# A convolution's last input load, issued later and with its last 16 partitions cut into short and long pieces

## Chip, cores and metric

The kernel runs on one core of one Trainium2 chip. The metric is device time in microseconds (us), median over executions; lower is better. A profiled span is about 1.7 us shorter than the same execution's time. A run is called slow, and left out of medians and ratios below, when it is over 1.5% above the fastest of its kernel.

## The reference

A 3x3 convolution, padding 1, 16 images of 64 channels and 64x64 pixels, 128 output channels, all float32; 9 of 10 weights are zero.

```python
x_pad = np.pad(x, ((0, 0), (0, 0), (pad, pad), (pad, pad)), mode='constant')
for b, co, ci, kh, kw in ...:            # five nested loops
    if weight[co, ci, kh, kw] != 0:
        output[b, co] += weight[co, ci, kh, kw] * x_pad[b, ci, kh:kh+h, kw:kw+w]
```

## The kernel before

Two images ("a pair") fill the 128 partitions: 64 channels each. GpSimd issues the loads of x, converted to bf16 on the way, all at the start; SyncE issues the stores. For each block of 16 image rows GpSimd (POOL in the profiles) makes a sum `s` (three buffers), PE, the matrix engine, multiplies, VectorE (DVE) adds and writes the output tile.

```python
nc.sync.dma_start(out=w_sb, in_=weight...)
nc.sync.dma_start(out=x_head[:, 0:HEAD, :], in_=pair(0)[:, 0:HEAD, :])
nc.gpsimd.dma_start(out=xs[0][:, HEAD:H, :], in_=pair(0)[:, HEAD:H, :])
...
for p in range(1, NP):                                   # NP = 8 pairs
    nc.gpsimd.dma_start(out=xs[p], in_=pair(p))
# ... weights, 27 idle matmuls, first conversions (cut)
for p in range(NP):
    o = [o_pool.tile([C_OUT, H, W], FP32, name="o") for _ in range(2)]
    last = p == NP - 1
    for blk in range(4):
        ...                                              # GpSimd, PE, ACT, VectorE
        if last and blk % 2 == 1:                        # last pair: stores by halves
            for n in range(2):
                rows = slice(r0 - 16, r0 + 16)
                nc.sync.dma_start(out=out[2 * p + n][:, rows, :], in_=o[n][:, rows, :])
    if not last:
        for n in range(2):
            nc.sync.dma_start(out=out[2 * p + n], in_=o[n])
```

## Time and profile before

| | before |
|---|---|
| time, median | 127.66 us (3 runs, 127.59 to 127.9) |
| profiled span | 125.4 us |
| PE's unbroken stretch | 7.12 to 109.21 us |
| last compute step ends | 111.76 us |
| last store lands | 124.20 us |

The row to read is the last one against the one above it: 12.4 us in which only DMA engines work. Two more lines of the page are needed later. The first counts packets of the DMA queues by size; those under 512 B are nearly all 4-byte completion increments. The second gives, for the seven whole loads of x, the size and the time from issue to landing:

```profile
DMA packets 4044, 42.93 MB, mean 342 GB/s; under 512 B 448, under 2 KB 448, under 8 KB 704
...
x<-in_x_dram POOLq DMA_DIRECT2D x7, 1024.0 KB, 29.3
```

### The profile page before, as it was taken

What the parts mean: (1) busy time and instruction counts of PE and PEld (TensorE: products, weight loads), DVE (VectorE), ACT (ScalarE), POOL (GpSimd) and SP (SyncE); (2) the same over time, 40 slices, a digit from 0 to 9 for tenths busy, and PEclk for the clock granted to TensorE, in tenths of its full rate; (3) what the DMA queues carried; (4) which work ended last, traced back from release to release, by engine and by line L of the source; (5) the groups of instructions that cost most, each with busy time, mean ns of one, the idle gap of its engine ahead of it and who ended that gap; (6) DMA issues with size and microseconds to landing.
All of it is one profiled execution on the core that took longest, in us unless ns stands there. A gap on an engine that the chain in (4) does not pass through costs nothing.

```text
span 125.4 us, 2486 instructions
## 1 busy us (share of the span) xinstructions
PE 107.5 (86%) x1002; PEld 58.8 (47%) x1002; DVE 82.4 (66%) x135; ACT 39.0 (31%) x71; POOL 40.7 (32%) x45
## 2 busy tenths in 40 slices
PE   6679999999999999999999999999999999920000
PEld 6435555555555555555555555555555555500000
DVE  0463877877787778777877787778777877760000
ACT  4555323333333333333333333333333333300000
POOL 6936533333333333333333333333333300000000
PEclk9999999999999999999999999999999999997555
DMA  5999999989999999999999999999999999999980
GB/s 146 338 222 220 212 214 220 191 259 350 324 311 337 308 293 319 342 316 308 426 429 423 408 429 434 450 416 434 418 418 429 429 444 423 434 397 423 423 369 10
DMA packets 4044, 42.93 MB, mean 342 GB/s; under 512 B 448, under 2 KB 448, under 8 KB 704
## 3 DMA queue, kind: packets, MB, share of 16 engines
q1 hardware_dynamic: 2880, 34.90, 66.2%
q0 software_dynamic: 1152, 7.86, 30.7%
q8 instruction: 8, 0.13, 0.4%
q14 instruction: 4, 0.03, 0.1%
HBM read 17.07 MB, written 33.55 MB: 404 GB/s over the span
## 4 chain that ended last, share of the span: by engine, by line
PE 81%; DMA 4%; DVE 1%; issue 1%; DVEq 0%; SPq 0%
PE ps L135 81%; DMA o<-in_x_dram 4%; DVE o L168 1%; DVEq L214 0%; DVE x L87 0%; SPq L60 0%; DVEq L168 0%
## 5 line engine op out<-in xcount | busy, mean ns | idle before, releaser
L168 DVE TENSOR_TENSOR o<-ps,pc 128x512 f32<-128x512 f32 x124 | 77.8, 686 | 22.1 <-PE ps L135 19.8
L135 PE MATMUL ps<-x,wT 64*128 64x504 bf16 (+3 forms) x780 | 88.8, 373 | 1.5 <-DVE x L87 1.5
L135 PEld LDWEIGHTS <-wT 64*128 64x128 bf16 x966 | 55.2, 94 | 49.4 <-issue 1.5
L154 POOL TENSOR_TENSOR s<-x 128x512 bf16<-128x512 bf16 x31 | 35.6, 1152 | 57.7 <-PE ps L135 41.5
L161 ACT COPY pc<-ps 128x512 f32<-128x512 f32 x62 | 33.3, 589 | 64.0 <-issue 61.8
L135 PE MATMUL ps<-s,wT 64*128 64x512 bf16 (+1 forms) x186 | 25.7, 377 | 0.0
L74 PE MATMUL ps<-idle_rhs 128*128 128x128 bf16 x27 | 3.1, 310 | 1.0 <-DVE idle_rhs L71 1.0
L67 POOL DMA_DIRECT2D x<-in_x_dram x7 | 3.7, 561 | 0.0
L74 PEld LDWEIGHTS <-idle_rhs 128*128 128x128 bf16 x27 | 2.8, 144 | 1.0 <-DVE idle_rhs L71 1.0
L91 DVE CAST w_bf<-w_sb 128x192 bf16<-128x192 f32 (+1 forms) x4 | 1.3, 382 | 3.0 <-DMA w_sb<-in_weight_dram 3.0
L149 DVE COPY o<-ps 128x512 f32<-128x512 f32 x2 | 1.4, 692 | 2.0 <-PE ps L135 2.0
L148 ACT COPY o<-ps 128x512 f32<-128x512 f32 x2 | 1.2, 586 | 2.4 <-PE ps L135 2.4
L87 ACT CAST x<-o 128x576 bf16<-128x576 f32 (+1 forms) x2 | 1.5, 802 | 0.5 <-DMA o<-in_x_dram 0.5
L91 ACT ACT_TABLE_LOAD x1 | 1.3, 1283 | 0.7 <-PEq L203 0.7
L97 PE MATMUL ps<-ident,w_bf 128*128 128x128 bf16 x9 | 1.1, 292 | 0.4 <-DVE w_bf L91 0.4
L87 DVE CAST x<-o 128x576 bf16<-128x576 f32 x1 | 0.5, 460 | 1.4 <-DMA o<-in_x_dram 1.4
L91 ACT CAST w_bf<-w_sb 128x64 bf16<-128x64 f32 (+1 forms) x2 | 0.7, 418 | 1.9 <-DMA w_sb<-in_weight_dram 1.9
L97 PEld LDWEIGHTS <-w_bf 128*128 128x128 bf16 x9 | 0.8, 128 | 0.8 <-DVE w_bf L91 0.8
L101 DVE TENSOR_TENSOR wT<-ps,wT 128x384 bf16<-128x384 f32 x2 | 1.0, 550 | 0.0
L63 POOL DMA_DIRECT2D x<-in_x_dram x1 | 0.7, 696 | 0.8 <-POOLq L203 0.8
L71 DVE MEMSET idle_rhs<- 128x64 uint32 x1 | 0.1, 112 | 0.8 <-PEq L203 0.8
L110 ACT CAST wT<-ps 128x384 bf16<-128x384 f32 x1 | 0.5, 481 | 0.4 <-PE ps L97 0.4
(8 smaller groups left out, 1.9 us busy)
## 6 DMA issues: line engine op xcount, KB each, us to landing
out_dram<-o SPq DMA_DIRECT2D x14, 2048.0 KB, 19.8
x<-in_x_dram POOLq DMA_DIRECT2D x7, 1024.0 KB, 29.3
out_dram<-o SPq DMA_DIRECT2D x4, 1024.0 KB, 12.3
o<-in_x_dram SPq DMA_DIRECT2D x1, 1024.0 KB, 5.4
x<-in_x_dram POOLq DMA_DIRECT2D x1, 512.0 KB, 7.5
w_sb<-in_weight_dram SPq DMA_DIRECT2D x1, 288.0 KB, 3.1
```

Of the source, the lines that this page charges most:

```text
L67: nc.gpsimd.dma_start(out=xs[p], in_=pair(p))
L74: nc.tensor.matmul(idle_ps, idle_rhs, idle_rhs, start=True, stop=True)
L87: copy(out=xs[0][:, a:b, :], in_=x_head[:, a:b, :])
L91: copy(out=w_bf4[:, g, a:b, :], in_=w_v[:, k : k + b - a, :])
L97: nc.tensor.matmul(wps[:, j, :], src, ident, start=True, stop=True)
L101: nc.vector.tensor_tensor(out=wT[:, g], in0=wps, in1=wT[:, G1], op=SUB)
L135: nc.tensor.matmul(ps[n][:, lo:hi, c_lo:c_hi], tap(g, kw, n), src[q, a:b:step, c_lo + kw - 1 : c_hi + kw - 1], start=(i == 0), stop=(i == ...
L148: nc.scalar.copy(out=o[0][:, r0 : r0 + rows, :], in_=ps[0])
L149: nc.vector.tensor_copy(out=o[1][:, r0 : r0 + rows, :], in_=ps[1])
L154: nc.gpsimd.tensor_tensor(out=s, in0=xs[p][:, r0 : r0 + 16 : 2, :], in1=xs[p][:, r0 + 1 : r0 + 16 : 2, :], op=ADD)
L161: nc.scalar.copy(out=c, in_=shared[n])
L168: nc.vector.tensor_tensor(out=o[n][:, first : r0 + 16 : 2, :], in0=ps[n], in1=pc[n], op=ADD)
```

## The change

The 16 DMA engines do not end together. As I read it, the change means to give engines 0 to 7 a little less of the last load and engines 8 to 15 a little more; it also issues this load later.

```diff
-    for p in range(1, NP):
+    for p in range(1, NP - 1):
         nc.gpsimd.dma_start(out=xs[p], in_=pair(p))
...
     for p in range(NP):
         o = [...]
+        if p == 2:
+            for c0, c1, a, b in (
+                (0, 112, 0, H),
+                (112, 120, 0, 8),
+                (112, 120, 8, H),
+                (120, 128, 0, 8),
+                (120, 128, 8, H),
+            ):
+                nc.gpsimd.dma_start(
+                    out=xs[NP - 1][c0:c1, a:b, :], in_=pair(NP - 1)[c0:c1, a:b, :]
+                )
```

## The prediction

> **What bounds the kernel now.** I read the page's slices first, then the chain that ended last, then stretches by stage, then the data queues at the end. The slices show two things busy from start to finish: the PE and the transfers. Only one of them reaches the end.
>
> ```profile
> span 125.4 us, 2486 instructions
> ...
> PE   6679999999999999999999999999999999920000
> ...
> DMA  5999999989999999999999999999999999999980
> ...
> q1 hardware_dynamic: 2880, 34.90, 66.2%
> q0 software_dynamic: 1152, 7.86, 30.7%
> ```
>
> PE falls idle in slice 36 of 40 (about 110 us); the 16 DMA engines stay at nine tenths or more two to three slices longer. The two queues, q1 (stores, and the first two loads) and q0 (the other loads of x, converted to bf16 on the way), take 66.2% + 30.7% = 96.9% of all 16 engines' time over the whole span. The chain of waits agrees: its last compute step is a VectorE add that ends at 111.16 + 0.60 = 111.76 us, though the span is 125.4; what follows is only the landing of stores.
>
> ```profile
> 7.12 102.09 PE ps L135 x954
> ...
> 111.16 0.60 DVE o L168
> ```
>
> By stage (columns: stretch, its length, busy time of each engine, granted clock, DMA share, GB/s):
>
> ```profile
> 25.00:53.00 28.00, 28.00 (x264) 14.98 (x262) 21.72 (x36) 9.30 (x18) 10.10 (x9) 1.00 1.01 317
> 63.00:109.00 46.00, 46.00 (x432) 24.58 (x430) 35.81 (x58) 16.10 (x30) 13.84 (x12) 1.00 1.01 429
> 112.00:122.00 10.00, 0.00 (x0) 0.00 (x0) 0.00 (x0) 0.00 (x0) 0.00 (x0) 0.63 0.97 409
> 122.00:125.40 3.40, 0.00 (x0) 0.00 (x0) 0.00 (x0) 0.00 (x0) 0.00 (x0) 0.50 0.05 19
> ```
>
> The last row but one is 10 us in which nothing computes and the DMA engines run at 0.97. The last pair's second half, 2 x 1024 KB, becomes ready at 111.8; at 429 GB/s it alone would need 2.1 MB / 429 = 4.9 us. It lands 12.4 us after that, so some 7.5 us of the tail are backlog. The kernel is bound by the total work of its DMA queues, and the PE has slack of that size.
>
> The last row is what the change can touch: a few engines are still moving data when most have stopped. Closer, 119 to 125 us (40 slices of 0.15 us):
>
> ```profile
> DMA  9697999999997977593922010101010000000000
> GB/s 601 273 546 328 492 382 492 382 437 437 437 437 328 382 328 328 218 382 164 382 109 109 0 55 0 55 0 55 0 55 0 0 0 0 0 0 0 0 0 0
> ```
>
> The alternation of 55 and 0 GB/s is one engine alone with one 8 KB packet after another. The trace has each engine's completion of the last store, which counts to 16: 121.28 for the first, then 121.33, 121.37, 121.58, 121.81, 122.18, 122.43, eight between 122.54 and 122.84, and the last at 124.20. Their mean is 122.35: perfect balance would be worth 1.85 us and no more. From single records I also see why there is a straggler: from 63 to 111 us the 16 KB store packets take 611 ns on 15 engines, but on one engine 634 to 662, mean 648 (75 packets, 37 ns extra each, 2.8 us in all). Before 63 us, where loads and stores alternate, I find no such packets.
>
> **What the Trainium skill says.** "Perfetto Trace Analysis", section What "DMA-bound" means, lists specific DMA engines as one of the ways to be DMA-bound; the single engine above is just that. "DMA: Bandwidth & Descriptors", section Queues, rings and completion order, says that each engine alternates between the queues that have work, a packet at a time; the trace agrees (from 26 to 60 us the packets of q0 and q1 alternate at 624 ns each). The same page, Why a DMA increments its semaphore by 16, says that a GpSimd-issued transfer runs on the largest number k up to 16 that divides its slowest dimension, k below 16 meaning k consecutive engines from a cursor that goes round, and that all 16 engines post an increment whatever the shape. By this, pieces of 8 partitions land alternately on engines 0 to 7 and 8 to 15. It also names an exception, in which k stays 16 with partitions/16 rounded up for each engine. The kernel before has only transfers of 128 partitions, so its trace shows neither. The same page, Latency and other measured facts, says that engines 7 and 15 are usually slower and guesses at the rings of GpSimd's queue. The trace has one slow engine, not two, and its records carry no engine number.
>
> **The change part by part.** (1) *Moving the issue.* The last load was issued at 5.6 us and landed 57.2 us later, at 62.8: it waited behind pairs 1 to 6 in its queue, and pair 6 landed at 53.0. Issued from within pair 2, after pair 1's last GpSimd add (start 21.57, 1.15 us, so from about 22.7), it still queues behind pair 6 and starts at the same 53 us. Worth nothing by itself. Five issues of 557 ns take 2.8 us of GpSimd, so pair 2's first add starts at about 25.5 instead of 24.72; the PE uses it only at 30.22 (the third product of s after the one that released it), and the add takes 1.15, so 3.5 us of slack remain. The 557 ns freed at 5.6 us buy nothing either: GpSimd next waits for ScalarE until 8.21. I take it that the point is to keep four extra issues (2.2 us) out of the start.
>
> (2) *Splitting the last 16 partitions.* Before, each engine moves 8 partition rows of the last pair, 8 x 624 ns. After, 112 partitions give each engine 7. The pieces give engines 0 to 7 two short rows (8 of 64 image rows, 1 KB written) and engines 8 to 15 two long ones (7 KB). In the records, a load row of 4096 B written takes 324 ns and one of 8192 takes 624, so a row costs about 24 ns + 73 ns per KB: 99 for a short one, 537 for a long one. Consecutive packets start 4 ns before the previous one ends. Four more completion increments per engine at 15.5 ns: 62 ns.
> - engines 0 to 7: -620 + 2 x 95 + 62 = -0.37 us
> - engines 8 to 15: -620 + 2 x 533 + 62 = +0.51 us
>
> No engine is ever idle between 8 and 121 us, so these shifts carry through to its last completion. If the straggler is one of 0 to 7: it ends at 124.20 - 0.37 = 123.83, and the latest of the others, even if it is among 8 to 15, at 122.84 + 0.51 = 123.35. The end comes 0.37 us earlier: 127.66 - 0.37 = 127.29.
>
> **The rivals.** *The straggler is among 8 to 15:* the end comes 0.51 later, 128.17. For it: the trace before doesn't say which engine is slow. Against: whoever made this change gave 0 to 7 the short rows, which makes sense only if those were seen to be late. *The exception on k holds for the small pieces,* and all four go to engines 0 to 7: these get 2 x 95 + 2 x 533 + 62 - 620 = +0.70, the others -0.56. With the straggler among 0 to 7 the end is at 128.4, otherwise at about 127.1. For it: the page says so of some copies. Against: the change is built on the cursor. *The end does not move,* because the profile's straggler is partly of the profiling, or because another engine takes its place: 127.6 to 127.8. For it: the slowness ends at 111 us, as soon as the compute does. *A GpSimd or PE wait on the five pieces:* against it stand the 3.5 us above and the 26 us between the landing of the load (62.8) and the first GpSimd add on pair 7 (88.75).
>
> **Range and chances.** I give the first case 0.6, the straggler in the other half 0.15, the exception 0.1, no movement 0.15. The middle lies a little above the main case: 127.35. The range takes in both halves for the straggler and some of the run-to-run spread (127.59 to 127.9 before): 126.9 to 128.2. Nothing in this sum reaches 2% (2.55 us), not even perfect balance at 1.85 us, so within 2% gets 0.97; the rest is for surprises in how GpSimd makes the small transfers.
>
> **What would show it.** Right: the landing of the last load's five transfers, 8 engines leaving the loads about 0.9 us before the other 8; the last completion of the last store near 123.8 with the second-last near 123.2; the PE's unbroken stretch still about 102 us. The slow engine should keep its 37 ns. Wrong: a last completion later than 124.2; GpSimd's add of pair 2 late enough for a PE gap near 30 us; a span that falls by over 1 us, which would mean that the order of work on the queues, which I hold to be unchanged, matters.

## The result, and the profile after

| | before | after |
|---|---|---|
| time, median | 127.71 us (127.59 to 127.9, 4 runs) | 128.05 us (127.84 to 128.24, 4 runs) |
| ratio, 95% interval | 1 | 1.0025 [1.0003, 1.0047] |

A ratio is the mean time of one kernel's fast runs over that of the other's of the same rounds, so it is not quite the ratio of the medians. The small difference has the sign opposite to my main case: 0.3 us slower, not 0.37 us faster.

The page of the kernel after, span, slices and queues:

```profile
span 126.4 us, 2494 instructions
...
PE   6569999999999999999999999999999999950000
...
PEclk9986999999999999999999999999999999999555
DMA  4999999999999999999999999999999999999960
...
DMA packets 4156, 42.93 MB, mean 340 GB/s; under 512 B 544, under 2 KB 560, under 8 KB 832
...
q1 hardware_dynamic: 2880, 34.90, 65.7%
q0 software_dynamic: 1264, 7.87, 30.7%
```

The DMA engines are the bound as before, at 65.7% + 30.7%. The chain of waits has PE ending 1.9 us later than before, and the tail from 119 us on has again one engine alone at the end:

```profile
7.38 103.77 PE ps L135 x954
...
113.10 0.60 DVE o L168
```

```profile
DMA  8999999989989694733223101011010000000000
GB/s 354 531 399 399 443 399 487 443 354 487 399 354 399 266 399 177 310 133 133 89 89 133 44 0 44 0 44 44 0 44 0 0 0 0 0 0 0 0 0 0
```

The last store's completions end at 123.69 and 125.22. I had forecast 123.2 and 123.8.

It is tempting to blame PE: PEclk, the granted clock, falls to 8 and 6 tenths in slices 3 and 4. By stage, 8 to 12 us, first of before, then of after (the third figure from the end is the granted clock):

```profile
8.00:12.00 4.00, 4.00 (x40) 2.13 (x38) 1.85 (x4) 1.52 (x4) 3.36 (x3) 1.00 1.04 217
```

```profile
8.00:12.00 4.00, 4.00 (x24) 1.81 (x22) 1.41 (x3) 0.96 (x2) 3.36 (x3) 0.57 1.06 221
```

PE did 24 matmuls in 4 us where it had done 40. But it happens to the unchanged kernel too. A control run of it (`f1_before`, below) shows the same dip, with a span of 126.4 us, as long as that of the changed kernel:

```profile
8.00:12.00 4.00, 4.00 (x30) 1.82 (x28) 1.52 (x3) 1.07 (x2) 3.36 (x3) 0.68 1.03 214
```

So the two profiles of this section differ by 1.0 us while the timed runs differ by 0.3. The profile of before was a lucky execution (127.12 us, faster than all four of its timed runs). What the pair of profiles alone suggests as to time is worth nothing here.

The clue is in the packet count. Four more transfers with 16 increments each make 64 more small packets. The page has 544 - 448 = 96.

### The profile page after: what moved, and what is told of

Same layout as the page of the kernel before. It is cut to its first block, busy times and chain, and to the rows that moved or that the text cites. A ratio compares the mean times of both kernels' runs of the same rounds, so it can differ in the third digit from the quotient of the medians.

```text
span 126.4 us, 2494 instructions
## 1 busy us (share of the span) xinstructions
PE 109.0 (86%) x1002; PEld 59.2 (47%) x1002; DVE 82.2 (65%) x135; ACT 38.9 (31%) x71; POOL 42.8 (34%) x49
## 3 DMA queue, kind: packets, MB, share of 16 engines
q1 hardware_dynamic: 2880, 34.90, 65.7%
q0 software_dynamic: 1264, 7.87, 30.7%
## 4 chain that ended last, share of the span: by engine, by line
PE 82%; DMA 4%; DVE 1%; issue 1%; DVEq 0%; SPq 0%
PE ps L135 82%; DMA o<-in_x_dram 4%; DVE o L168 1%; DVEq L227 0%; DVE x L87 0%; SPq L60 0%; DVEq L168 0%
## 5 line engine op out<-in xcount | busy, mean ns | idle before, releaser
L135 PE MATMUL ps<-x,wT 64*128 64x504 bf16 (+3 forms) x780 | 90.5, 378 | 2.1 <-DVE x L87 2.1
L67 POOL DMA_DIRECT2D x<-in_x_dram x6 | 3.2, 559 | 0.0
L185 POOL DMA_DIRECT2D x<-in_x_dram x5 | 2.6, 528 | 0.0
L63 POOL DMA_DIRECT2D x<-in_x_dram x1 | 0.7, 710 | 0.8 <-POOLq L216 0.8
```

The lines of the kernel that those rows point to most:

```text
L135: nc.tensor.matmul(ps[n][:, lo:hi, c_lo:c_hi], tap(g, kw, n), src[q, a:b:step, c_lo + kw - 1 : c_hi + kw - 1], start=(i == 0), stop=(i == ...
L185: nc.gpsimd.dma_start(out=xs[NP - 1][c0:c1, a:b, :], in_=pair(NP - 1)[c0:c1, a:b, :])
```

## The experiments

Twelve runs were made, in four jobs, each on a chip of its own; kernels of one job share the chip and the runs of before. Theories: A, the late engine is in the half that the change loads more; B, the five transfers cost time wherever they go; C, PE's clock in the profiled run; D, the later issue; then E, all pieces land on the same eight engines; M and P, on the cost of small packets. In single records I followed each engine by the rule that a packet starts 4 ns before the engine's previous one ends (18 or 19 ns after a row that is not whole).

### Does it matter which half gets the long pieces?

`e1_swap`:

```diff
-                (112, 120, 0, 8),
-                (112, 120, 8, H),
-                (120, 128, 0, 8),
-                (120, 128, 8, H),
+                (112, 120, 8, H),
+                (112, 120, 0, 8),
+                (120, 128, 8, H),
+                (120, 128, 0, 8),
```

> The changed kernel with the two pieces of each pair in the other order: long first, so that the half of the DMA engines that got the long rows now gets the short ones. Theory A (the one late engine lies in the half that the change loads more): that engine now does 0.37 us less than before, so about 127.3 us, ratio to before 0.997. Rival B (the change costs time by its five transfers, whoever gets which): as the changed kernel, ratio 1.0025. Rival C (the profile's difference is the PE's lower clock and later end in that run): ratio 1.000 to 1.0025 and no link to the order. In the trace theory A wants the last completion about 0.37 us closer to the mean of the 16 than in the kernel before (1.85 us above it there).

Measured: 128.07 us, ratio 1.0023 [1.0010, 1.0037] (one run of 130.51 was slow and is left out). Theory A is out: it wanted 0.997.

`e2_even`, four pieces of 32 image rows:

```diff
-                (112, 120, 0, 8),
-                (112, 120, 8, H),
-                (120, 128, 0, 8),
-                (120, 128, 8, H),
+                (112, 120, 0, 32),
+                (112, 120, 32, H),
+                (120, 128, 0, 32),
+                (120, 128, 32, H),
```

> The changed kernel with the four pieces all of 32 image rows, so that every engine gets the same. Only the cost of five transfers in place of one is left: two packets of 320 ns for one of 620, and four more completion increments of 15 ns, +0.08 us by the sum of the prediction. Theory A: 127.8, ratio 1.0006. Rival B: ratio 1.0025, like the changed kernel. Rival C: no forecast.

Measured: 128.13 us, 1.0026 [1.0014, 1.0038]. Short-long, long-short and even all cost the same 0.3 us. Theory B had this right, but so has a theory that I had listed as a rival in the prediction: if all four pieces go to the same engines, their lengths and order cannot matter.

### Does the later issue cost anything?

`e3_move`, the last load in one piece, from within pair 2:

```diff
-                (0, 112, 0, H),
-                (112, 120, 0, 8),
-                (112, 120, 8, H),
-                (120, 128, 0, 8),
-                (120, 128, 8, H),
+                (0, 128, 0, H),
```

> Only the first half of the change: the last load in one piece, issued from within pair 2. Theory A: nothing, ratio 1.000, with pair 7's load landing at about 62.8 us as before, since it still queues behind pair 6. Rival D (the later issue itself costs, by moving GpSimd's descriptor work into the time when the stores begin): ratio about 1.0025.

Measured: 127.75 us against 127.78; the ratio over all six runs is 1.0023 [0.9983, 1.0063], widened by the first, profiled one of 129.51. The other five lie between 127.65 and 127.77. The profile of the first shows what went with it: the very first load landed 3 us late, so PE's stretch started at 10.16 us instead of about 7.4, and PE's clock was low as well.

```profile
1.17 8.45 DMA o<-in_x_dram
...
10.16 104.47 PE ps L135 x954
```

In the other five runs moving the load is worth nothing, as predicted.

### Number of transfers, or the engines they land on?

`f1_before` is the kernel before once more, as a control.

> The kernel before, unchanged, as a control, since its one profiled execution (span 125.4 us) was faster than any of its eleven timed ones in the last job (125.7 to 126.2). Ratio 1.000. Its trace should show again one engine 1.3 us or more behind the next, after store packets of about 648 ns, with a span nearer 126.0.

Measured: 127.81 us, 1.0016 [0.9994, 1.0038], so the noise of such a comparison is 0.1 to 0.2%, and the 0.25% of the changed kernel is barely clear of it. What supports that figure is that swap and even repeat it. Its trace has the late engine again, 1.5 us behind the next (125.22 after 123.71), and 58 of its store packets between 55 and 100 us at a mean of 648 ns; the changed kernel has 57, at 648.

`f2_sixteen` keeps five transfers, but each piece has all 16 partitions:

```diff
-                (112, 120, 0, 8),
-                (112, 120, 8, H),
-                (120, 128, 0, 8),
-                (120, 128, 8, H),
+                (112, 128, 0, 16),
+                (112, 128, 16, 32),
+                (112, 128, 32, 48),
+                (112, 128, 48, 64),
```

> Five transfers as in the changed kernel, but the four pieces have all 16 partitions and 16 image rows each, so all 16 engines get one row of each. Theory E (pieces of 8 partitions all run on the same 8 engines, among them the late one, so those carry 9 rows of the last pair where they had 8, and swapping or evening the pieces changes nothing): this removes the imbalance, +0.1 us by packet costs (4 x 166 + 62 - 620 ns), ratio 1.001, and no ladder of empty increments in the trace. Rival B (the number of transfers costs the time): ratio 1.0025 as in the changed kernel.

Measured: 127.5 us, 0.9985 [0.9966, 1.0005], without one slow run of 131.21. The repeat, `f2b_sixteen`:

> The even split into pieces of 16 partitions once more, since its interval [0.9966, 1.0005] took in 1. Theory M: 0.9985 again. Theory P: 1.001. Rival B (the number of transfers costs): 1.0025.

Measured: 127.71 us, 1.0003 [0.9982, 1.0024], again without one slow run (129.8). Five transfers, issued at the same place, cost nothing measurable when every engine gets a share. Theory B is out in both, in the second by a hair.

`f3_double` makes the pieces whole:

```diff
-                (0, 112, 0, H),
-                (112, 120, 0, 8),
-                (112, 120, 8, H),
-                (120, 128, 0, 8),
-                (120, 128, 8, H),
+                (0, 96, 0, H),
+                (96, 104, 0, H),
+                (104, 112, 0, H),
+                (112, 120, 0, H),
+                (120, 128, 0, H),
```

> 96 partitions in one transfer and four pieces of 8 whole partitions. Under the intent of the change (8 consecutive engines from a cursor) every engine gets 6 + 2 = 8 rows and nothing moves: ratio 1.0005. Theory E: 8 engines get 6 + 4 = 10 rows and 8 get 6; the late engine does 2 x 620 + 62 ns more, +1.3 us, ratio 1.010; scaled by what the changed kernel showed (half of its 0.70) it would be 1.005. Rival B (four more transfers cost 0.35 us wherever they go): 1.0025.

Measured: 128.76 us, 1.0089 [1.0068, 1.0111], +1.1 us. The cursor would have made this kernel balanced. Theory E forecast +1.3 us. This is the run that decides: with the rule of a cursor each engine gets eight rows and the time cannot move.

The packet counts tell a part of this without any timing. The kernels with pieces of 16 (first line, from the profile of its slow run) and with four whole pieces of 8 (second):

```profile
DMA packets 4156, 42.93 MB, mean 332 GB/s; under 512 B 512, under 2 KB 512, under 8 KB 832
```

```profile
DMA packets 4140, 42.93 MB, mean 339 GB/s; under 512 B 544, under 2 KB 544, under 8 KB 800
```

512 is 448 + 64, one increment on each engine for each of four transfers. 544 has 32 more, which fits 4 x 8: in every piece of 8 partitions, the eight engines without a share have one more 4-byte packet each. The count does not say whether these are the same eight in every piece; the cursor could give the same 544. The single records of the changed kernel show where they are. On exactly eight engines the 4-byte packets of the load queue follow one another every 613 ns, six to eight in a row, with one store packet between each two and never a data packet. Here is one of these ladders (start in us):

```
57.932  58.545  59.158  59.771  60.384  60.997  61.610  62.223
```

Two packets a piece and four pieces make eight. Under the cursor, no engine could have such a ladder, since each would have two pieces of data. So eight engines get all four pieces, and eight get none. Such ladders are in the traces of `e1_swap`, `e2_even` and `f3_double` too, and none is in that of `f2_sixteen`.

The exception is not the only reading of this: a cursor that starts anew with each transfer would place the pieces the same way, and no run tells the two apart.

### Is the late engine among those eight?

The records answer it directly. Followed back from its slow stores, the late engine of the changed kernel has load packets of 7168 B at 61.10 us, of 1024 B at 59.79 and of 7168 B at 58.02; that of `e1_swap` has 1024 B at 61.30, 7168 B at 59.54 and 1024 B at 58.23. With the cursor an engine would have got only short pieces or only long ones. So the late engine is one of the eight.

Stores can say more of its number, since for them the Trainium skill's page "DMA: Bandwidth & Descriptors" (section Why a DMA increments its semaphore by 16 and not by 1) says that the k engines of a transfer are the lowest-numbered k. `e4_store15` and `f4_spare7` cut only the very last store of the kernel before:

```diff
-                    nc.sync.dma_start(out=out[2 * p + n][:, rows, :], in_=o[n][:, rows, :])
+                    parts = ((0, 120), (120, 128)) if blk == 3 and n == 1 else ((0, 128),)
+                    for a, b in parts:
+                        nc.sync.dma_start(out=out[2 * p + n][a:b, rows, :], in_=o[n][a:b, rows, :])
```

> The kernel before; only its very last store (1 MB) is split into 120 + 8 partitions, which by the Trainium skill's rule on k runs on engines 0 to 14 with 8 rows each and then on 0 to 7 with one row more each. If the late engine is number 15, it is spared 8 packets of 309 ns, 2.45 us, and the end is set by another engine at 122.84 + 0.31 = 123.15 us instead of 124.20: ratio 0.992. If the late engine is any other of 8 to 14: no change, 1.000. If it is one of 0 to 7: +0.31 us, ratio 1.0025.

Measured: 128.01 us, 1.0033 [1.0013, 1.0052]. That is the forecast for a late engine among 0 to 7 (1.0025). The number of increments agrees with k: 15 + 8 in the trace in place of 16. The completions of the 8-partition piece end at 123.29, 123.89 and 124.68, and the last of these follows the last of the 120 partitions (124.38) by 0.30 us, one packet: the late engine.

`f4_spare7` has the same edit with cuts at 0, 112, 119, 126, 128.

> The kernel before; its very last store (1 MB) is cut into 112 + 7 + 7 + 2 partitions. By the rule on k for stores (lowest-numbered engines) engines 7 to 15 move 7 rows of it instead of 8, engines 2 to 6 move 9, engines 0 and 1 move 10. If the late engine is number 7 of the lowest eight, its end comes 0.31 us earlier and the others stay below it: ratio 0.9975. If it is one of 2 to 6: +0.31 us, 1.0025; if 0 or 1: +0.61 us, 1.005.

Measured: 128.12 us, 1.0036 [1.0014, 1.0057]. Both pieces of 7 end with one completion far behind the rest (125.13 after 122.83, 125.42 after 123.13); the piece of 2 was done at 122.11 and 122.43. So the late engine is one of those that the page would number 2 to 6. It is not 7.

`g2_spare4`, cuts at 0, 112, 116, 120, 124, 128:

> The kernel before; its very last store is cut into 112 + 4 x 4 partitions. By the rule on k for stores engines 4 to 15 move 7 of its rows instead of 8 (-0.31 us) and engines 0 to 3 move 11 (+0.92). The two earlier cuts put the late engine among numbers 2 to 6. If it is 4, 5 or 6: it ends 0.31 us earlier, and 0 to 3 end near 123.6: ratio 0.9975, better than both kernels. If it is 2 or 3: +0.92 us, ratio 1.007.

Measured: 127.68 us, 1.0001 [0.9969, 1.0032]. The tail, first of before and then of this kernel, both from 119 us:

```profile
DMA  9998989896949496747311010101000000000000
```

```profile
DMA  9879999949696989699360524242211000000000
```

The long end of one engine alone is gone. The 112-partition part ends at 124.44, the next engine at 123.79; the last piece of 4 ends at 124.26 to 124.82. So the late engine has none of these pieces and is 4, 5 or 6 by that numbering, if it is the same engine on the three chips that these cuts ran on, which no run tests. It was relieved, but the four engines that took its share end at 124.82 in this trace, not at the 123.6 that I had worked out from the profile of before, whose second-last engine ended at 122.84 (123.71 in the control). There is no gain.

### What limits the pieces, and can small packets help?

Five-transfer kernels came out a little better than the sum of their packets (below). Theory M was that the late engine's stores are slow only where no load packet comes between. `g1_eight` was to give more turns to the load queue:

```diff
-                (112, 120, 0, 8),
-                (112, 120, 8, H),
-                (120, 128, 0, 8),
-                (120, 128, 8, H),
+                (112, 128, 0, 8),
+                ...                                   # eight pieces of 8 image rows
+                (112, 128, 56, 64),
```

> As the even split into pieces of 16 partitions, but eight pieces of 8 image rows. By packet costs alone: 8 x 95 + 8 x 15.5 - 620 ns = +0.26 us, ratio 1.002 (theory P). Theory M (the late engine's store packets take 648 ns only where no load packet, however small, comes between them; each extra turn of the load queue, data or increment, lets one of its stores run at 611 to 620 ns): 23 turns in the last pair where the kernel before had 9, so up to 14 x 33 ns = -0.46 us on the late engine, in all -0.2 us, ratio 0.9985; the first slow store packets come later in the trace than in the kernel before, by the time of some 14 store packets where the stores start at the same time.

Measured: 151.78 and 153.26 us in the two runs that count as fast, ratio 1.1933 [1.1862, 1.2005]; the other four took 154.68 to 155.96. Nothing in either theory foresaw this. GpSimd's timeline in the profiled run, one of the slower ones (start, length, what, and the idle time before with what ended it):

```profile
22.63 2.51 POOL L189 DMA_DIRECT2D x<-in_x_dram  x5
33.51 0.48 POOL L189 DMA_DIRECT2D x<-in_x_dram  x1 [8.37 <-DMA x<-in_x_dram]
43.32 0.48 POOL L189 DMA_DIRECT2D x<-in_x_dram  x1 [9.33 <-DMA x<-in_x_dram]
53.10 0.48 POOL L189 DMA_DIRECT2D x<-in_x_dram  x1 [9.30 <-DMA x<-in_x_dram]
61.66 0.48 POOL L189 DMA_DIRECT2D x<-in_x_dram  x1 [8.08 <-DMA x<-in_x_dram]
62.16 4.46 POOL L154 TENSOR_TENSOR s<-x 128x512 bf16<-128x512 bf16 x4
```

Five issues pass, then each waits for the landing of an earlier load. GpSimd's transfers use eight completion semaphores in turn (eight count in the trace, numbers 99 to 106), and a ninth transfer must wait until the first has landed. GpSimd makes no sum meanwhile, and PE waited 29.8 us for it in one go:

```profile
PE ps L135 <- POOL s L154: 29.8, 1, 29.8
```

This suggests what the late issue in the change is for, though no run issued all twelve transfers at the start. With seven loads issued at the start, transfers 8 to 12 go out at 24.6 us, when the four semaphores that they take over are just free (pair 3's load landed by 24.25 in that trace). GpSimd in the kernel after:

```profile
24.61 2.57 POOL L185 DMA_DIRECT2D x<-in_x_dram  x5
27.18 1.17 POOL L154 TENSOR_TENSOR s<-x 128x512 bf16<-128x512 bf16 x1
29.91 1.15 POOL L154 TENSOR_TENSOR s<-x 128x512 bf16<-128x512 bf16 x1 [1.55 <-PE ps L135]
```

No wait. The delayed sum, the eighth of the kernel, was used by PE's eighth product of a sum at 35.32 us, 7.0 us after it was done.

`g3_seven` asks the question of `g1_eight` without the wait: from within pair 5, one transfer of 112 partitions and seven of 16.

```diff
-        if p == 2:
+        if p == 5:
...
-                (112, 120, 0, 8),
-                (112, 120, 8, H),
-                (120, 128, 0, 8),
-                (120, 128, 8, H),
+                (112, 128, 0, 10),
+                (112, 128, 10, 19),
+                ...                                   # seven pieces of 9 or 10 image rows
+                (112, 128, 55, 64),
```

> The same question as the run with eight pieces, whose GpSimd stalled: its sixth to ninth transfers each waited for the landing of an earlier load, as if only eight transfers of GpSimd could be outstanding (eight semaphores, used in turn). Here the last load goes out from within pair 5 (about 61 us), when pair 6's load has landed (53 us), in one transfer of 112 partitions and seven of 16 partitions and 9 or 10 image rows: eight in all, so no wait if that reading is right, and no PE gap. By packet costs alone +0.23 us, ratio 1.002 (theory P). Theory M (turns of the load queue relieve the late engine's stores): 22 turns in place of 9, up to -0.43 us, in all -0.2 us, ratio 0.9985. If GpSimd stalls again, the reading of eight semaphores is wrong.

Measured: 127.5 us, 0.9975 [0.9957, 0.9993], and no wait:

```profile
63.24 3.95 POOL L188 DMA_DIRECT2D x<-in_x_dram  x8
```

The reading of eight semaphores stands. P, which wanted 1.002, is out. M gets its sign: no slow store packet appears between 70 and 80 us, while this load is moving. But the number of slow packets falls only from 77 in the control to 74, about 0.1 us, against 0.43 forecast. The run also differs from the others in its place (pair 5), which I did not try with one piece. So this kernel is some 0.3 us faster than the kernel before, the best ratio, and the cause is not settled.

## Why the prediction was right or wrong

The measured 128.05 us lies in the range of 126.9 to 128.2 and within 2% as forecast. But the main case was wrong, and that the range held is luck: by the prediction's own sum, the rival that came true ends at 128.4, outside the range, and its cost came out at half of that sum.

**The bound: right, but PE's slack was put too high.** The queues are full to the end in the profiles of before, the control and after. With PE's stretch ending 1.9 us later in the control than in before (111.09 against 109.21), the last store landed 1.0 us later (125.22 against 124.20), so the prediction's slack of some 7.5 us is not free; why the tail moves by half is not settled. In `e3_move`'s first run, with PE's stretch ending at 114.6 us, the DMA engines fell to 4 tenths in a slice near 104 us and the time rose to 129.51.

**The moved issue: right as to time, incomplete as to purpose.** It is worth 0.0 us (five runs of `e3_move`). I took it to spare the start four issues, 2.2 us. The runs suggest a larger reason: the limit of eight transfers, which in `g1_eight` cost some 25 us. One reading was wrong without harm: the sum made at 24.72 us in before, the eighth, is used by PE at 33.38 us, not at 30.22, so that 6.7 us of slack remained and not 3.5.

**"By this, pieces of 8 partitions land alternately on engines 0 to 7 and 8 to 15": this step failed.** They all land on one set of eight engines, shown by the eight ladders, by the late engine's own packets (both 1024 B and 7168 B) and by the ratio of 1.0089 in `f3_double`. With it fell "-0.37" for one half and "+0.51" for the other. Swapping and evening made no difference (1.0023, 1.0026, 1.0025).

**The placement of the second rival, "the exception on k holds for the small pieces", is what happened;** I had given it 0.1. The trace of before could not tell, having only transfers of 128 partitions; yet the page names the exception, and the guess that whoever wrote the change had checked the cursor was no evidence. That the late engine is in the set that gets the pieces is shown by its own packets and by the loss in `f3_double`. The numbers 4 to 6 rest on the page's rule for stores, since the records carry none.

**The size of that rival was off by half.** Its sum, +0.70 us, gave 128.4; measured were +0.32 (0.0025 x 127.7), and +0.29 and +0.33 for swap and even. With twice the pieces the sum of +1.30 was nearly right (+1.14). With pieces of 16 it was +0.10, measured -0.19 and +0.04. All fall short by 0.1 to 0.4 us, for the changed kernel, swap and even by more than their intervals, so the sum of packet durations overstates what a small extra transfer in the load queue costs the late engine. Theory M explains the sign; its count of slow packets explains a part only. This stays open.

**The late engine itself: right.** It is there in every trace read packet by packet, with 648 ns where the others take 611. That its lateness is only of the profiling does not fit `g2_spare4`: four engines had 0.92 us more to store there, which would have cost a ratio of 1.007 had no other engine ended that much later, and the timed runs show 1.0001, at most 1.0032. The sign that I had named, a last completion later than 124.2, says nothing: the unchanged kernel has it too (125.22 in the control).

## What to carry to other kernels

Before relying on which DMA engines a narrow transfer runs on, test it with one kernel that would be balanced if the rule held and clearly slower if not; swapping two pieces is a cheap second test. Count completion packets on the profile page: with the timing hidden in noise they hint at how many engines took part; which ones, only the single records tell. And count outstanding transfers of one issuing engine against its completion semaphores before adding more, since the issue of one too many can stall that engine's compute as well.

## What the Trainium skill lacked or had wrong

- "DMA: Bandwidth & Descriptors", section Why a DMA increments its semaphore by 16 and not by 1: the round-robin cursor for k below 16 did not show in any run here. These converting loads of 8 partitions, issued by GpSimd, were placed as by the exception in all four kernels that have them: every piece on the same eight engines, with ladders of eight empty turns on the others, and 1.0089 for a kernel that the cursor would have balanced. The page names the exception for "some direct copies" (100 and 127 partitions) without saying when it applies.
- Same section: it does not say that an engine without a share posts a second 4-byte packet beside its increment; here 32 for four pieces. For stores the rule of the k engines agreed with the trace (15 + 8 increments for 120 + 8 partitions).
- Same page, section Latency and other measured facts: it has engines 7 and 15 slower and calls it specific to GpSimd's queue. Here one engine was slow, in stores of SyncE's queue (648 ns for 16 KB against 611), mainly while no loads ran and until the compute ended at 111 us, and by the store cuts, with the page's rule on k for them, it is one of numbers 4 to 6 (if the same on all chips).
- On none of the pages that I looked up: the limit of eight outstanding GpSimd transfers in this program, where each later issue waited 8.1 to 9.3 us for an earlier load, and GpSimd's compute with it.
